# Scan phases moved among the outer products, x rows and raw weights asked for by ScalarE, bias products moved to the end of the first half

## The chip, the cores and the metric

The kernel runs on one core of one Trainium2 chip. The metric is the device time of one execution in microseconds; a figure for a kernel is the median of its runs. The profiled execution has a time of its own, given beside its span (first to last instruction). PE is TensorE (PEld its weight loads), DVE VectorE, ACT ScalarE, POOL GpSimd, SP SyncE, which here only starts transfers (SPq).

## The reference, cut to what matters

One layer of a hybrid decoder on 2048 tokens of width 1024. Only its first part is touched by the change: the RMSNorm of x, the combined projection, the tables that the state-space mixer is scanned with, and the vectors of the relative bias.

```python
h = rms_norm(x, norm1_g)                     # per token: x * rsqrt(mean(x*x) + eps) * g
P = h @ w_in                                 # 1024 x 1676, columns of groups A, u and C
A_bar = jnp.exp(A * dt)                      # 32 groups x 64 complex states
B_bar = ((A_bar - 1.0) / A)[..., None] * Bm
_, states = lax.associative_scan(_scan_combine, (a_seq, Bu), axis=1)
bias = bias_tbl[rel_bucket(dist)]            # for every distance, 8 heads
```

After it come the local and compressed attention, the output projection and a feed-forward part of width 4096, which the change leaves as they are, but for how one pool of tiles is declared.

## The kernel before, in words

All large products are made in three passes of a high and a low word (`mm3`, L81 to 85). `phase_front` (L94 to 303) makes the projection in two halves of 1024 tokens. Each half first makes the 512 columns of u, transposed (`u_step`, twice 96 matmuls of 512 columns), and then three chunks of columns, a, b and c (384, 384 and 396 wide), each for 8 tiles of 128 tokens: one `product` (L178) is 24 matmuls into one of two banks of PSUM (`ps_m`). ACT takes a bank out, scaled by the token's RMS factor `rx` (L190), and squares a part (L192), DVE sums the squares (L193), and POOL stores the row (L194). A product can start when the bank of the one before the last is out.

The factors `rx` come from `row_sum` (L115): a row of x of 512 KB is loaded and ACT sums its squares (L120). Rows 0 to 7 are loaded by SP during the second u step. Rows 8 to 15 are asked for by POOL, one after each product of chunk a: POOL copies one column of the evicted tile into the row's tile (L118) so that the load (L119) comes behind the eviction. `row_factors` (L122) makes 8 factors on DVE.

The raw weights of a chunk go through 3 buffers (`fetch_w`, L141, on SP) and are split by ACT (L154) and DVE (L155) in `keep_w`; for a, b and c of the first half these two are given a higher priority (`W_HOIST`, 300), so that the scheduler puts them early.

`ssm_tables` (L357) is a generator whose parts are merged between the steps of u and of chunk a. On DVE it makes powers 0 to 16 of the decay by one exponential over 17 x 32 values per partition (L399 and `exp_acc`), the sines (ACT, L349), the powers of the rotation, then the scan phases `Ea` and `Eb` by doubling (L431 to 446), and the matrices Y and W. `pair_steps` (L508) then makes, 16 times, an outer product on DVE (L519 to 521), a product on PE (`pk`, L528) and their stores; its steps are merged between the rest of a, b and c. The phases are first read in `table_steps` (L561), in the second half.

`bias_vectors` (L785) runs between the two parts of chunk a in program order: SP loads the table (`tab`) and six pieces of a one-hot matrix (`boh`), PE multiplies them (`bpr`, L797), ACT copies the result out and POOL stores it. Its tiles lie in a pool `bv` of their own, on memory that the tables' temporary tiles used before. `bias_rows` (L803) later spreads the result over 128 rows of DRAM (`rsw`, `r2w`, 5.1 MB written). At the start of the second half `rx` is turned by PE and written out (L227 to 231), and read back as `rxb` for the evictions of u.

Within `phase_front` the program order is a hint: a scheduler orders each engine's instructions at build time by its own estimate of when they can start, and the order is then fixed. Each engine and each queue works strictly in order.

Of the kernel before, what the change touches and what calls it, by code (L numbers as in the profile page):

```python
# [16 lines left out]
P = 128  # L17
# [76 lines left out]
def phase_front(tc, C, x, norm1_g, w_in, uT, pd, rh_a, prm, ssm_d, rx_d, consts, extra, later, x_t, r_last, last_bank):  # L94

    nc = tc.nc
    with ExitStack() as ctx:
# [15 lines left out]
        def row_sum(t, after=None):  # L113
            xr = rp.tile([P, D], F32, tag="x", name=f"x{t}", bufs=3)
            if after is None:  # L115
                nc.sync.dma_start(xr, xv[t])
            else:
                nc.gpsimd.tensor_copy(xr[:, 0:1], after)  # L118
                nc.gpsimd.dma_start(xr, xv[t])  # L119
            nc.scalar.activation(xr, xr, AF.Square, accum_out=ss[:, t:t + 1])  # L120

        def row_factors(half):  # L122
            sl = slice(8 * half, 8 * half + 8)
            with tc.high_priority(offset=W_HOIST):
                rsqrt_into(nc, rp, rx[:, sl], ss[:, sl], 1.0 / D, 8, "rq")

# [22 lines left out]
        def keep_w(half, kind, c0, n, k, raw):  # L149
# [3 lines left out]
            with tc.high_priority(offset=W_HOIST) if kind in "abc" and not half else nullcontext():  # L153
# [22 lines left out]
        open_, box_x, w_more = {}, [], []  # L176

        def product(t, hs, w, kind, c0, n, part=None):  # L178
# [29 lines left out]
        for half in range(2):  # L208
# [17 lines left out]
            if half:  # L226
                ptr = ps_t.tile([P, 512], F32, tag="pt", name="ptr")[0:NT, 0:P]  # L227
                nc.tensor.transpose(ptr, rx, C["ident"])
                rxt = sm.tile([NT, P], F32, tag="rxt", name="rxt", bufs=1)
                nc.scalar.copy(rxt, ptr)  # L230
                nc.gpsimd.dma_start(rx_d.rearrange("n r c -> (n r) c"), rxt)
                tables = table_steps(tc, C, S, ctx.enter_context(tc.tile_pool(name="sgt", bufs=1, side="right", reuse_waits="tile")), ps_t)
            c_x = ctx.enter_context(ExitStack())
            with tc.tile_pool(name=f"a_psu{half}", bufs=1, space=PSUM, reuse_waits="tile") as ps_u:
# [30 lines left out]
                if half == 0:  # L265
# [3 lines left out]
                    sums = [lambda t=t: row_sum(t) for t in range(8)] + [lambda: row_factors(0)]  # L269
# [9 lines left out]
            if half == 0:  # L279
                with tc.tile_pool(name="sg_ps0", bufs=1, space=PSUM, reuse_waits="tile") as ps_g:  # L280
# [76 lines left out]
def ssm_tables(tc, C, S, pool, first, prm, dkp):  # L357
# [17 lines left out]
    S.update(Y=Y, Yp=Yp, W=W, C1=C1, C2=C2, AR=AR, AI=AI, Ea=Ea, Eb=Eb, rho16=rho16, dD=dD)  # L375
# [4 lines left out]
    with ExitStack() as ctx2:  # L380
        tp2 = ctx2.enter_context(tc.tile_pool(name="si2", bufs=1))
        with ExitStack() as ctx:
# [11 lines left out]
            jt = C["ramp"]  # L394
            xr = tmp([P, 17, G], "xr")
# [3 lines left out]
            nc.vector.tensor_tensor(xr, adr.unsqueeze(1).broadcast_to([P, 17, G]), jt.unsqueeze(2).broadcast_to([P, 17, G]), op=ALU.mult)  # L399
            yield  # L400
            rho = exp_acc(nc, tp, xr, [P, 17, G], "e2")
            yield
            nc.vector.tensor_copy(rho16, rho[:, 16])
# [4 lines left out]
            sincos(nc, k, sc, th)  # L408

# [19 lines left out]

            yield  # L430
            nc.vector.tensor_scalar(sn[64:P, 4:11], sn[64:P, 4:11], -1.0, None, op0=ALU.mult)  # L431
            for E, j0, m in ((Eb, 4, 4), (Ea.rearrange("p g j a -> p j g a")[:, 1:3], 8, 3)):
                nc.vector.memset(E[:, 0, :, 0:1], 1.0)
                nc.vector.memset(E[:, 1, :, 0:1], 0.0)
                for j in range(m):
                    n = 2 ** j
# [2545 lines left out]
```

## Time and profile before

| | |
|---|---|
| median of 3 runs | 2428.22 us (2425.92 to 2432.09) |
| profiled execution | 2422.61 us, span 2420.8 us |
| PE busy | 2360.3 us, 97% of the span |
| DVE, ACT, POOL busy | 74%, 53%, 45% |
| mean granted clock of TensorE | 0.992 |

The whole kernel is bound by PE, so time is gained only where PE waits or runs at its lower clock. The granted clock is given as a share of 2.4 GHz: 1.00 is the upper level and 0.50 the lower one (1.2 GHz). The first half of the projection lies between 0 and 192 us of the span.

### The profile page before, as it was taken

Reading aid. Unit: us, or ns where it says so; the run is one execution under the profiler, and the core shown is the slowest. Engines: PE = TensorE matmul, PEld = TensorE weight load, DVE = VectorE, ACT = ScalarE, POOL = GpSimd, SP = SyncE. Lnnn points to the kernel's source line nnn. Section 1 sums busy time; section 2 is a strip of 40 time slices with the busy share of each in tenths; the row PEclk is TensorE's granted clock in tenths of the full one; section 3 lists DMA queues with packets and bytes.
Section 4 is the critical chain, followed back from the end, with each engine's and each line's share of the span. In section 5 each row is a group of like instructions: output and inputs, shape, how many; then the busy total and the mean of one; then the engine's idle time right before and its main releaser. Section 6 shows DMA issues by size and latency. Waiting matters only on the chain. (4 is left out here: it accounts for less than half of the span.)

```text
span 2420.8 us, 37163 instructions
## 1 busy us (share of the span) xinstructions
PE 2360.3 (97%) x12292; PEld 2019.6 (83%) x12292; DVE 1782.6 (74%) x3470; ACT 1294.4 (53%) x2726; POOL 1087.2 (45%) x1210
## 2 busy tenths in 40 slices
PE   8899999999899999999999999999999999999999
PEld 7798999787788889888788888888877888888887
DVE  7866885885877888886855557545567888888886
ACT  5443545775777676665655555544454344433442
POOL 1331122323443454332676665566562554545547
PEclk9899999999999999999999999999999999999999
DMA  8674554641322343112666677655548444344435
GB/s 269 179 253 140 179 157 144 168 151 53 129 75 79 92 120 118 43 56 96 196 205 195 195 217 215 191 158 147 148 145 272 135 130 123 100 138 133 128 102 197
DMA packets 409766, 361.60 MB, mean 149 GB/s; under 512 B 45132, under 2 KB 360290, under 8 KB 407492
## 3 DMA queue, kind: packets, MB, share of 16 engines
q1 hardware_dynamic: 355460, 295.83, 40.5%
q10 hardware_dynamic: 43296, 34.09, 4.5%
q0 software_dynamic: 10816, 29.31, 3.6%
q8 instruction: 97, 1.59, 0.3%
q14 instruction: 97, 0.79, 0.1%
HBM read 236.31 MB, written 128.02 MB: 150 GB/s over the span
## 5 line engine op out<-in xcount | busy, mean ns | idle before, releaser
L2228 ACT CAST v<-vr 128x512 fp32r<-128x512 f32 x224 | 139.4, 624 | 295.7 <-DMA vr<-vd 139.7
L2229 DVE TENSOR_TENSOR v<-vr,v 128x512 fp32r<-128x512 f32 x224 | 237.9, 1071 | 80.2 <-ACT v L2228 79.2
L2392 DVE TENSOR_TENSOR ul<-fs,uh 128x512 fp32r<-128x512 f32 x124 | 112.2, 923 | 104.7 <-ACT uh L2391 104.5
L2694 PE MATMUL pdc<-dw,v 128*128 128x512 f32 x768 | 184.9, 389 | 2.6 <-DVE acc L2715 2.6
L2694 PE MATMUL pda<-dw,v 128*128 128x512 f32 x768 | 184.8, 389 | 0.7 <-ACT acc0u L2700 0.7
L2694 PE MATMUL pdb<-dw,v 128*128 128x512 f32 x768 | 184.8, 389 | 0.0
L2694 PEld LDWEIGHTS pdc<-dw,v 128*128 128x128 f32 x768 | 144.0, 188 | 33.3 <-DVE acc L2715 3.4
L2694 PEld LDWEIGHTS pda<-dw,v 128*128 128x128 f32 x768 | 144.1, 188 | 31.0 <-ACT acc0u L2700 1.1
L2694 PEld LDWEIGHTS pdb<-dw,v 128*128 128x128 f32 x768 | 144.1, 188 | 30.3 <-DVE acc L2715 0.4
L2391 ACT CAST uh<-fs 128x512 fp32r<-128x512 f32 x124 | 74.3, 620 | 160.0 <-POOL fs L2380 123.2
L2392 DVE TENSOR_TENSOR ul<-ur,uh 128x512 fp32r<-128x512 f32 x93 | 87.9, 948 | 68.5 <-ACT uh L2391 68.5
L2539 POOL TENSOR_TENSOR ev<-ex,e 128x512 f32<-128x512 f32 x32 | 43.1, 1347 | 206.7 <-ACT ex L2522 206.7
L1662 ACT CAST ths<-pps 128x512 fp32r<-128x512 f32 (+1 forms) x144 | 79.0, 564 | 72.2 <-PE pps L1646 63.2
L2522 ACT ACTIVATE e<-e 128x512 f32<-128x512 f32 x128 | 81.0, 633 | 53.4 <-DVE e L2491 51.4
L1667 DVE TENSOR_TENSOR tls<-pps,ths 128x512 fp32r<-128x512 f32 (+1 forms) x144 | 92.6, 657 | 23.0 <-ACT ths L1662 22.2
L1997 PE MATMUL pw<-wo_h,mh 128*128 128x512 f32 x256 | 106.6, 416 | 1.2 <-DVE mx L2019 0.9
L2470 PE MATMUL pub<-fh,uh 128*128 128x512 f32 x256 | 101.7, 397 | 4.9 <-DVE e L2491 4.9
L1997 PE MATMUL pw<-wo_h,ml 128*128 128x512 f32 x256 | 104.6, 409 | 0.0
L1997 PE MATMUL pw<-wo_l,mh 128*128 128x512 f32 x256 | 104.2, 407 | 0.0
L2470 PE MATMUL puc<-fl,uh 128*128 128x512 f32 x256 | 99.8, 390 | 1.6 <-DVE fl L2410 1.5
L2470 PE MATMUL pub<-fh,ul 128*128 128x512 f32 x256 | 100.6, 393 | 0.0
L2470 PE MATMUL puc<-fh,ul 128*128 128x512 f32 x256 | 99.8, 390 | 0.7 <-DVE ul L2392 0.7
(581 smaller groups left out, 7604.0 us busy)
## 6 DMA issues: line engine op xcount, KB each, us to landing
vr<-vd SPq DMA_DIRECT2D x224, 256.0 KB
ur<-in_w_up SPq DMA_DIRECT2D x124, 256.0 KB
vd<-ev SPq DMA_DIRECT2D x96, 256.0 KB
vd<-e ACTq DMA_DIRECT2D x64, 256.0 KB
dr<-in_w_down SPq DMA_DIRECT2D x32, 512.0 KB
mx<-in_x ACTq DMA_DIRECT2D x32, 256.0 KB
x<-mx ACTq DMA_DIRECT2D x32, 256.0 KB
vd<-e SPq DMA_DIRECT2D x32, 256.0 KB
```

Of the source, the lines that this page charges most:

```text
L1662: yield "ACT", cast_ns(n), lambda: nc.scalar.copy(th[:, 0:nb], pt[:, 0:nb])
L1667: t = yield "DVE", sub_ns(n), lambda: nc.vector.tensor_tensor(tl[:, 0:nb], pt[:, 0:nb], th[:, 0:nb], op=ALU.subtract)
L1997: t = yield "PE", mm_ns(512), lambda: nc.tensor.matmul(pw[n], a[half][:, j], b[k][:, sl], start=k == 0 and m == 0, stop=k == NK - 1 and m ...
L2228: nc.scalar.copy(dh, src)
L2229: nc.vector.tensor_tensor(dl, src, dh, op=ALU.subtract)
L2391: yield "ACT", 621, lambda: self.nc.scalar.copy(h, src.tile)
L2392: t = yield "DVE", 900, lambda: self.nc.vector.tensor_tensor(l, src.tile, h, op=ALU.subtract)
L2470: nc.tensor.matmul(banks[b], w[:, j], h[:, j], start=k < 4 and j == 0 and i == 0, stop=j == HALF - 1 and i == 2, skip_group_check=True)
L2522: t = yield "ACT", 640, lambda: nc.scalar.activation(r, r, func)
L2539: t = yield "POOL", 1400, lambda: nc.gpsimd.tensor_tensor(E["v" + q].tile, E[x].tile, E[y].tile, op=op)
L2694: nc.tensor.matmul(bank[b, q], x[:, q, j], y[:, j], start=first and j == 0 and n == 0, stop=j == 1 and n == 2, skip_group_check=True)
```

## The change

The scan phases leave `ssm_tables` and become nine steps (`phase_steps`) that are merged over the later part of the outer products. The 17 powers of the decay come from one exponential of 32 values and four doublings. Rows 8 to 15 of x are asked for by ACT after the products of chunk b, and each is summed one product later. The first three raw weights of chunk b are loaded behind the first eviction of chunk a, and the split of b's weights loses its priority. The one-hot matrix is loaded by ACT in three pieces of up to 1024 columns into row tiles, and the bias products, five now, come among the last three products of chunk c. The turning of `rx` moves ahead of them. In `phase_down` five tiles of split weights are declared as one pool of five buffers instead of five pools' places.

```diff
-        def row_sum(t, after=None):
-            xr = rp.tile([P, D], F32, tag="x", name=f"x{t}", bufs=3)
+        def row_tile(name):
+            return rp.tile([P, D], F32, tag="x", name=name, bufs=3)
+        def row_load(t, after=None):
+            xr = x_row[t] = row_tile(f"x{t}")
             if after is None:
                 nc.sync.dma_start(xr, xv[t])
             else:
-                nc.gpsimd.tensor_copy(xr[:, 0:1], after)
-                nc.gpsimd.dma_start(xr, xv[t])
+                nc.scalar.copy(xr[:, 0:1], after)
+                nc.scalar.dma_start(xr, xv[t])
+        def row_sum(t):
+            xr = x_row.pop(t)
             nc.scalar.activation(xr, xr, AF.Square, accum_out=ss[:, t:t + 1])
...
+        def turned_factors():
+            ptr = ps_t.tile([P, 512], F32, tag="pt", name="ptr")[0:NT, 0:P]
+            nc.tensor.transpose(ptr, rx, C["ident"])
...
             raw = pool.tile([P, n], F32, tag="wraw", name=f"wr{half}_{kind}{c0}_{k}", bufs=bufs)
+            if (kind, half) == ("b", 0) and k < 3:
+                nc.scalar.copy(raw[:, 0:1], newest[0])
...
-            with tc.high_priority(offset=W_HOIST) if kind in "abc" and not half else nullcontext():
+            with tc.high_priority(offset=W_HOIST) if kind in "ac" and not half else nullcontext():
...
+            newest.append(o[:, 0:1])
             store(1)
-            if (kind, t // 8) == ("a", 0):
-                row_sum(t + 8, o[:, n:n + 1])
+            if (kind, t // 8) == ("b", 0):
+                row_load(t + 8, o[:, 0:1])
+                if t:
+                    row_sum(t + 7)
...
+                    bvp = []
+                    fetch, products = extra(kf, bvp, ps_t)
...
-                    with tc.tile_pool(name="bv", bufs=1, reuse_waits="tile") as bv:
-                        extra(bv, ps_t)
                     pre = c_pre.enter_context(tc.tile_pool(name="pre", bufs=1, side="right", reuse_waits="tile"))
+                    bvp.append(pre)
                     pairs = pair_steps(tc, C, S, ssm_d, pre, ps_g)
-                    run(merge(l2[n2:] + [lambda: row_factors(1)] + lists[1] + lists[2], pairs))
+                    l3 = lists[2][:2] + [lambda: (row_sum(NT - 1), row_factors(1))] + lists[2][2:3] + [lambda f=f: f(row_tile) for f in fetch] + lists[2][3:5] + [turned_factors] + merge(lists[2][5:], products)
+                    run(merge(merge(l2[n2:] + lists[1] + l3), merge([lambda: None] * 10 + phase_steps(tc, S, pre)), pairs))
...
-            nc.vector.tensor_tensor(xr, adr.unsqueeze(1).broadcast_to([P, 17, G]), jt.unsqueeze(2).broadcast_to([P, 17, G]), op=ALU.mult)
-            rho = exp_acc(nc, tp, xr, [P, 17, G], "e2")
...
+            e = exp_acc(nc, tp, adr, [P, G], "e2")
+            nc.vector.memset(rho[:, 0], 1.0)
+            nc.vector.tensor_copy(rho[:, 1], e)
+            for n in (1, 2, 4, 8):
+                nc.vector.tensor_tensor(rho[:, n + 1:2 * n + 1], rho[:, 1:n + 1], rho[:, n:n + 1].broadcast_to([P, n, G]), op=ALU.mult)
...
+def phase_steps(tc, S, tp):
+    def double(E, j0, j):
+        t = tp.tile([P, GB, 17, 16], F32, tag="ot", name=f"et{j0}{j}", bufs=1)...
+        nc.vector.tensor_tensor(e1, E[:, 0, :, 0:n], er, op=ALU.mult)
+        (five more, as L441 to L445 before)
+    return [start] + [lambda E=E, j0=j0, j=j: double(E, j0, j) for E, j0, m in parts for j in range(m)] + [end]
...
-    res = [lambda: None] * 5
+    res = [lambda: None] * 1
...
-def bias_vectors(tc, tp, ps, rel_bias, oh2, ohs, r2, rs):
+def bias_vectors(tc, first, tp, ps, rel_bias, oh2, ohs, r2, rs):
+    tab = first.tile([33, 8], F32, name="b_tab", bufs=1)
+    def fetch(j, row):
+        o = M[j] = row(f"boh{j}")
+        m = min(D, n2 - j)
+        nc.scalar.dma_start(o[0:33, 0:m], oh2[:, j:j + m])
+        if m < D:
+            nc.scalar.dma_start(o[0:33, m:m + n1], ohs)
+    def part(c0):
+        nc.tensor.matmul(pr[0:8, 0:n], tab, M[c0 // D * D][0:33, c0 % D:c0 % D + n], start=True, stop=True)
...
+    return [lambda row, j=j: fetch(j, row) for j in range(0, n2, D)], [lambda j=j: part(j) for j in range(0, n2, 512)]
...
-        w_high = pool("d_w2", 1)
-        w_last = pool("d_w3", 1)
+        w_high = pool("d_w2", 5)
```

## Rows read from the trace of the kernel before

**Rows 1.** The page: its busy shares, and the granted clock by 40 slices of 60.5 us.

```profile
PE 2360.3 (97%) x12292; PEld 2019.6 (83%) x12292; DVE 1782.6 (74%) x3470; ACT 1294.4 (53%) x2726; POOL 1087.2 (45%) x1210
...
PEclk9899999999999999999999999999999999999999
```

**Rows 2.** What PE waited for between 50 and 130 us: us in total, times, longest.

```profile
PE bpr L797 <- DMA boh<-in_k_oh: 6.6, 2, 5.3
PE pm_a L83 <- ACT po_a L190: 3.3, 1, 3.3
```

**Rows 3.** Busy time of the engines in the three gaps of PE, each followed by the stretch behind it: length, busy time (instructions) of PE, PEld, DVE, ACT and POOL, granted clock, share of the DMA engines, GB/s.

```profile
61.90:65.36 3.46, 0.14 (x2) 0.00 (x1) 1.87 (x9) 3.43 (x6) 0.00 (x0) 0.83 0.61 147
65.36:71.10 5.74, 5.74 (x18) 5.74 (x19) 5.60 (x21) 2.98 (x6) 2.18 (x6) 0.51 0.57 151
93.30:98.69 5.39, 0.06 (x1) 0.03 (x1) 5.20 (x11) 3.14 (x7) 0.90 (x2) 0.97 0.60 156
98.69:105.30 6.61, 6.61 (x18) 4.79 (x19) 6.18 (x11) 3.74 (x9) 3.79 (x5) 0.51 0.69 200
112.70:114.05 1.35, 0.08 (x2) 0.03 (x1) 0.78 (x3) 1.35 (x4) 0.00 (x0) 1.00 0.58 149
114.05:120.40 6.35, 6.35 (x20) 4.17 (x20) 4.77 (x20) 1.88 (x5) 2.69 (x6) 0.73 0.47 179
```

**Rows 4.** The same columns for chunk a, from its first matmul to the second gap.

```profile
53.48:93.30 39.82, 36.51 (x193) 35.93 (x191) 35.10 (x130) 18.18 (x33) 9.18 (x20) 0.91 0.57 163
```

**Rows 5.** PE in order of time (start, duration): the first matmul of products a0 and a1, the first behind the first gap with what ended it, and two successive groups of pair products, each behind a product of chunk b.

```profile
53.48 0.33 PE L83 MATMUL pm_a<-wh_a,hh 128*128 128x384 f32 x1
57.69 0.35 PE L83 MATMUL pm_a<-wh_a,hh 128*128 128x384 f32 x1
65.36 0.69 PE L83 MATMUL pm_a<-wh_a,hh 128*128 128x384 f32 x1 [3.31 <-ACT po_a L190]
147.57 1.02 PE L528 MATMUL pk<-oCA,k_Y 128*128 128x256 f32 x4
152.60 1.02 PE L528 MATMUL pk<-oCA,k_Y 128*128 128x256 f32 x4
```

**Rows 6.** ACT in order of time around the first gap.

```profile
61.62 0.61 ACT L154 ACTIVATE wh_b<-wr_b,g 128x384 fp32r<-128x384 f32 x1 [5.84 <-DMA wr_b<-in_w_in]
62.25 1.28 ACT L349 ACT_TABLE_LOAD   x1
64.75 0.56 ACT L190 ACTIVATE po_a<-pm_a,rx 128x384 f32<-128x384 f32 x1
```

**Rows 7.** Transfers started by SP, and DVE in order of time, around the second gap; the third row is one of SP's waits between 50 and 130 us.

```profile
96.06 0.34 SPq L790 DMA_DIRECT2D tab<-in_rel_bias  x1
96.45 0.42 SPq L795 DMA_DIRECT2D boh<-in_k_oh  x1
...
SPq L790 <- DVE t_v L490: 25.1, 1, 25.1
...
95.35 0.68 DVE L490 TENSOR_TENSOR t_v<-t_B,k_qi 128x512 f32<-128x512 f32 x1
98.44 0.07 DVE L789 MEMSET tab<- 1x8 f32 x1
```

**Rows 8.** The matmuls of the bias products, from the view of their tile: duration in ns least, median, most; first and last start.

```profile
L797 PE MATMUL bpr<-boh,tab x12: 482/522/921, 98.7 to 123.1; 33*8 33x432 f32 x10, 33*8 33x384 f32 x2
```

**Rows 9.** DVE: the exponential's two longest groups with 544 values, the same with 32 values, and the first and the last instruction of the scan phases (43 in all).

```profile
L321 DVE TENSOR_TENSOR e2t<-e2p,e2r x6: 725/726/726, 39.0 to 47.0; 128x544 f32<-128x544 f32 x6
L322 DVE TENSOR_SCALAR e2p<-e2t x6: 435/444/444, 41.6 to 49.9; 128x544 f32<-128x544 f32 x6
L321 DVE TENSOR_TENSOR e1t<-e1p,e1r x6: 129/191/193, 27.4 to 30.3; 128x32 f32<-128x32 f32 x6
...
77.63 0.20 DVE L440 TENSOR_TENSOR t_tp<-k_Eb,k_sc 128x32 f32<-128x32 f32 x1
92.49 0.28 DVE L446 TENSOR_SCALAR k_Ea<-k_Ea 128x256 f32<-128x256 f32 x1
```

**Rows 10.** The x rows: ACT's wait for them between 50 and 130 us, and the time from issue to landing (least, median, most) of the rows that POOL asks for; then the same of the stores `dca` of the outer products, which run from 106.6 to 171.9 us.

```profile
ACT x L120 <- DMA x<-in_x: 23.0, 7, 5.1
...
DMA to landing us min/median/max: 4.2/4.7/6.0
...
DMA to landing us min/median/max: 2.3/4.7/11.8
```

**Rows 11.** DVE in order of time: the first and the last instruction that make the factors of rows 8 to 15; the first waits for ACT's sum of row 15.

```profile
113.27 0.17 DVE L51 TENSOR_SCALAR rqh<-ss 128x8 f32<-128x8 f32 x1 [1.99 <-ACT x L120]
120.72 0.15 DVE L61 TENSOR_TENSOR rx<-rx,rqt 128x8 f32<-128x8 f32 x1
```

**Rows 12.** The first of the bias rows' four large transfers on SP (the other three follow from 137.37 us), the stretch of 25 us in which they run (columns as in Rows 3), ACT's longest wait for the weights of the second half behind them, the last split of the second half's x on DVE, and the first matmul of that half on PE.

```profile
126.00 0.52 SPq L806 DMA_DIRECT2D r2w<-r  x1
...
125.00:150.00 25.00, 25.00 (x140) 24.27 (x139) 15.26 (x30) 9.60 (x20) 9.65 (x18) 1.00 0.88 283
...
158.96 0.72 ACT L154 ACTIVATE wh_u<-wr_u,g 128x512 fp32r<-128x512 f32 x1 [5.13 <-DMA wr_u<-in_w_in]
182.88 1.23 DVE L129 TENSOR_TENSOR hl<-xT,hh 128x1024 fp32r<-128x1024 f32 x1 [1.54 <-ACT hh L128]
192.48 0.48 PE L83 MATMUL pu<-hh,wh_u 128*128 128x512 f32 x1
```

More of the change, by code (lines that the diff above doesn't have):

```diff
@@ L125, in row_factors @@
                 rsqrt_into(nc, rp, rx[:, sl], ss[:, sl], 1.0 / D, 8, "rq")
+        def turned_factors():
+            ptr = ps_t.tile([P, 512], F32, tag="pt", name="ptr")[0:NT, 0:P]
+            nc.tensor.transpose(ptr, rx, C["ident"])
+            rxt = sm.tile([NT, P], F32, tag="rxt", name="rxt", bufs=1)
+            nc.scalar.copy(rxt, ptr)
+            nc.gpsimd.dma_start(rx_d.rearrange("n r c -> (n r) c"), rxt)
         def half_words(h, l, raw):
@@ L226, in phase_front @@
             if half:
[L227 to L231, printed above, removed]
                 tables = table_steps(tc, C, S, ctx.enter_context(tc.tile_pool(name="sgt", bufs=1, side="right", reuse_waits="tile")), ps_t)
@@ L268, in phase_front @@
                     rp = c_rp.enter_context(tc.tile_pool(name="a_r", bufs=2, side="right", reuse_waits="tile"))
-                    sums = [lambda t=t: row_sum(t) for t in range(8)] + [lambda: row_factors(0)]
+                    sums = [lambda t=t: (row_load(t), row_sum(t)) for t in range(8)] + [lambda: row_factors(0)]
                     kf = c_rp.enter_context(tc.tile_pool(name="a_kf", bufs=1, side="right", reuse_waits="tile"))
@@ L498, in ssm_tables, with start, end @@
         nc.vector.tensor_tensor(dD, dT.unsqueeze(2).broadcast_to([16, G, 16]), C["ident"][0:16, 0:16].unsqueeze(1).broadcast_to([16, G, 16]), op=ALU.mult)
+def phase_steps(tc, S, tp):
+    nc = tc.nc
+    Ea, Eb, sn, cs = S["Ea"], S["Eb"], S["sc"][:, 0], S["sc"][:, 1]
+    parts = (Eb, 4, 4), (Ea.rearrange("p g j a -> p j g a")[:, 1:3], 8, 3)
+    def start():
+        nc.vector.tensor_scalar(sn[64:P, 4:11], sn[64:P, 4:11], -1.0, None, op0=ALU.mult)
+        for E, _, _ in parts:
+            nc.vector.memset(E[:, 0, :, 0:1], 1.0)
+            nc.vector.memset(E[:, 1, :, 0:1], 0.0)
+    def double(E, j0, j):
+        n = 2 ** j
+        t = tp.tile([P, GB, 17, 16], F32, tag="ot", name=f"et{j0}{j}", bufs=1).rearrange("p i t q -> p (i t q)")[:, 0:16 * G].rearrange("p (i n g) -> p i n g", i=2, g=G)
+        er = cs[:, j0 + j].unsqueeze(2).broadcast_to([P, G, n])
+        ei = sn[:, j0 + j].unsqueeze(2).broadcast_to([P, G, n])
+        e1, e2 = (t[:, i, 0:n].rearrange("p n g -> p g n") for i in range(2))
+        nc.vector.tensor_tensor(e1, E[:, 0, :, 0:n], er, op=ALU.mult)
+        nc.vector.tensor_tensor(e2, E[:, 1, :, 0:n], ei, op=ALU.mult)
+        nc.vector.tensor_tensor(E[:, 0, :, n:2 * n], e1, e2, op=ALU.subtract)
+        nc.vector.tensor_tensor(e1, E[:, 0, :, 0:n], ei, op=ALU.mult)
+        nc.vector.tensor_tensor(e2, E[:, 1, :, 0:n], er, op=ALU.mult)
+        nc.vector.tensor_tensor(E[:, 1, :, n:2 * n], e1, e2, op=ALU.add)
+    def end():
+        nc.vector.tensor_scalar(Ea[:, :, 0], Ea[:, :, 2], -1.0, None, op0=ALU.mult)
+    return [start] + [lambda E=E, j0=j0, j=j: double(E, j0, j) for E, j0, m in parts for j in range(m)] + [end]
 GB = 2
@@ L2762, in trunk @@
           cmp_pos, cmp_w1, cmp_w2, out_norm_g, w_out, norm2_g, w_up, w_down,
-          k_ident, k_ramp, k_oh2, k_ohs, k_blk, k_forced, k_wmask, k_rows31, k_sel, x_t, out, dbg=None):
+          k_ident, k_oh2, k_ohs, k_blk, k_forced, k_wmask, k_rows31, k_sel, x_t, out, dbg=None):
     nc = tc.nc
@@ L2775, in consts @@
             nc.sync.dma_start(C["ident"], k_ident)
-            for n, src in (("ramp", k_ramp), ("forced", k_forced), ("rows31", k_rows31)):
+            for n, src in (("forced", k_forced), ("rows31", k_rows31)):
                 C[n] = cp.tile(list(src.shape), F32, name="c_" + n)
@@ L2784, in consts, with biases @@
                 nc.vector.tensor_scalar(gains[:, j:j + 1], gains[:, j:j + 1], 0.125, None, op0=ALU.mult)
-        def biases(tp, ps):
-            bias_vectors(tc, tp, ps, rel_bias, k_oh2, k_ohs, r2, rs)
+        def biases(first, tp, ps):
+            return bias_vectors(tc, first, tp, ps, rel_bias, k_oh2, k_ohs, r2, rs)
         pd = {kind: dr.tile([L, n], F32, name="p" + kind) for kind, n in WIDTHS.items()}
```

58 lines of the change are left out of this document (18 added, 40 removed).

## The prediction

> **What bounds the kernel now.** I read the page first, then the waits of PE, then its stages. The page says that PE is busy for 97% of the span and that no other engine comes near [rows 1]: time is gained only where PE stands still or runs at its lower clock. In the clock line of the page a single digit, that of the second slice of 60.5 us, is below 9 [rows 1], so I asked for PE's waits between 50 and 130 us. There are three gaps there [rows 2]: one of 3.3 us for an eviction of chunk a, and two, 6.6 us in all, for the one-hot matrix of the bias products. The windows around them show the second half of the price [rows 3]: behind each gap the granted clock falls to the lower level, 1.2 GHz, though PE is busy without a break (5.74 us at 0.51, 6.61 us at 0.51, 6.35 us at 0.73). Chunk a agrees. One product takes 57.69 - 53.48 = 4.21 us at the upper level [rows 5], eight take 33.7 us, and the chunk took 39.82 us up to the second gap [rows 4]; the 6.1 us between are the first gap and the slow stretch behind it.
>
> Why the gaps are there is read from the other engines' order. First gap: product a2 needs the bank of a0, and ACT, which works in order, stood 5.84 us for raw weights of chunk b (put early by their priority), then loaded its table for the sine, and evicted a0 only at 64.75 us, 7 us after a0 was done at about 57.7 [rows 5, 6]. Second gap: the bias tiles lie on memory of the scan tables, so SP waited 25.1 us for DVE's last use of it (the instruction at 95.35), asked for table and matrix at 96, and DVE wrote the table's last row at 98.44 [rows 7]; PE, in order, had the bias product ahead of chunk b. Third gap: the fourth piece of the matrix came 1.3 us late [rows 2, 3].
>
> **The change part by part.**
>
> *First gap.* Without the priority, the split of b's weights no longer stands ahead of a0's eviction, and their first three loads come behind it by the copy on ACT. The sine moves ahead of the exponential, so ACT meets it some 15 us before a0 is done, where ACT waits for x rows anyway. The gap's 3.31 us go [rows 2], and with it the slow stretch: 5.74 x (1 - 0.51) = 2.8 us [rows 3]. What is late next? The weights of b are needed when chunk b starts, 33.7 us behind the start of a; the gate opens about 5 us into that time and eight loads through three buffers follow. In the trace a load that SP starts is split within a few us, so I cost this at nothing. If ACT waits for such a load ahead of the next eviction, it has one product, 4.2 us, before PE feels it.
>
> *Second and third gap.* The bias products go to the end of chunk c, their table is loaded early into memory of its own, and their matrix is asked for at least two products of c (over 8 us) ahead. The gaps' 6.6 us go [rows 2], and the slow stretches: 6.61 x 0.49 = 3.2 us and 6.35 x 0.27 = 1.7 us [rows 3]. The products themselves cost the same: 5 x 432 + 384 = 2544 columns before, 4 x 512 + 496 = 2544 after; 12 matmuls of 0.52 us are 6 us at most [rows 8], and the new ones the same by their columns. What comes later is `r2w` and `rsw`, below.
>
> *Exponential.* With 544 values a pair of its steps takes 0.73 + 0.44 us, with 32 values about 0.19 + 0.18 [rows 9]; over the 23 instructions and the product with the ramp that is about 13.8 us against 4.2, plus 1.3 for four doublings and copies: 8 us of DVE saved. DVE is not what PE waits for at that time, so I cost this at nothing; it only makes the tables earlier.
>
> *Scan phases.* 43 instructions, 77.6 to 92.8 us, with little between them [rows 9]: some 14 us of DVE leave chunk a and return among the outer products. There PE waits for no DVE result. DVE is busy for 15.26 of 25 us in the stretch of 125 to 150 us [rows 12], and the outer products start earlier by what left; no cost. If that cover were gone, the 14 us would delay the pair products, which nothing reads before the second half. The phases themselves are first read in the second half too.
>
> *x rows 8 to 15.* They move from POOL after a's products to ACT after b's. ACT loses 23.0 us of waiting [rows 10] that hid under chunk a. It gains eight issues, eight copies of one column (about 0.2 us each) and the same eight squares. A period of chunk b with its pair product is 152.60 - 147.57 = 5.0 us [rows 5]. By my estimate from these durations a row is asked for about 1.7 us after a product (eviction 0.56 [rows 6], square, copy, issue) and summed at about 2.2 us after the next, 5.5 us later; it lands in 4.7 us (4.2 to 6.0) [rows 10], so ACT waits for half a microsecond at most, against 4.2 us that it may be late. Cost nothing; bounds are nothing, and the case below in which the rows land late. The Trainium skill (DMA: Bandwidth & Descriptors, "Issuing engines are not separate DMA queues") speaks against a gain here: transfers started by any engine run on the same 16 DMA engines, and another issuer saves only the time to issue. By that rule 4.2 MB more share chunk b's stretch with the stores of the outer products, which land after 4.7 us and up to 11.8 us [rows 10]; no run shown has them together, and it is why I give the late landing below some chance.
>
> *Turned factors.* They wait for `row_factors(1)`, whose DVE chain took 113.27 to 120.87, 7.6 us [rows 11]. In the new order three products of c, 13 us, lie between the last row's sum and the transpose. That leaves some 4 us for the last row's landing and its sum; no cost.
>
> *Bias rows to DRAM.* 5.1 MB written in 126 to 145 us move behind the later bias products, some 25 to 40 us. They are 4 writes of 1.08 MB and 4 of 0.19 MB. Before, the DMA engines were at 0.88 in their stretch, and behind them ACT waited 5.13 us for a weight of the second half without PE feeling it [rows 12]. After, they meet the loads of the second half's x. The last of these was split at 184.1 us, and PE started that half at 192.48 [rows 12]: 8.4 us of slack against some 15 us of transfer that is shared. Bounds: nothing, or up to 7 us. I take 2 us, nearer to nothing, because SP's loads of x come first in program order.
>
> *Pool in `phase_down`.* Five tiles per chunk rotate over five buffers in the same order as before, each again in the same place: nothing.
>
> *Sum.* Gaps 3.3 + 6.6 = 9.9; clock 2.8 + 3.2 + 1.7 = 7.7; together 17.6 us less, 2 us given back: 15.6. The waits of PE after 250 us are for other engines' results, which move with it, so I let the whole shift reach the end. On the profiled execution that is 2422.6 - 15.6 = 2407.0 us; its time lies 5.6 us below the median of the runs shown, so the forecast for a median is 2428.2 - 15.6 = 2412.6, say 2412.
>
> **The rivals.**
>
> *B: the bias rows collide with the second half's loads.* For it: the 8.4 us of slack are less than the transfer, and the x loads go through few buffers. Against it: the first row of those waits was hidden before, and the scheduler may put the transfers later still. Price 7 us and a slow stretch of 2.8 us behind it: 2428.2 - 17.6 + 9.8 = 2420.4.
>
> *C: the first gap stays.* ACT could stand for b's weights (now loaded later) ahead of an eviction of chunk a, or for the sine. For it: ACT is in order, and 5.84 us is what it stood before [rows 6]. Against it: the split is now behind two evictions in program order. Then 6.1 us are not gained: 2428.2 - 15.6 + 6.1 = 2418.7.
>
> *D: the new places wait for transfers, and it gets slower.* The bias products, and the transpose ahead of them, stand in PE's order in chunk c behind three loads of the matrix on ACT's queue. These stand behind the sum of x row 15, and so behind that row's landing. It decides at a landing of about 8.5 us (two products of c): above that PE stands at each of the three pieces. If each costs what the second gap did, 5.34 + 3.2 us, that is 25.6 us: 2428.2 - 17.6 + 25.6 = 2436.2. For it: stores in that stretch landed in up to 11.8 us [rows 10], and rows of x are added. Against it: the 5.1 MB of bias rows leave just that stretch, and the median there is 4.7 us.
>
> **How the numbers follow.** Forecast (both kinds of gap go, little returns) 0.60; B 0.19; C 0.09; D 0.12. About 0.3%, 7.3 us here, is what a measurement can tell from no change. The forecast and C lie beyond it, B is on its edge (half and half), D is beyond it on the other side but for a sixth: faster 0.60 + 0.08 + 0.09 = 0.77, which I lower to 0.75 for what the scheduler does elsewhere with the same code; same 0.15; slower 0.10. The range starts at the full 17.6 us and the 2.3 us by which runs shown lie below their median, with some 3 us for cover that I did not see: 2405. It ends at 2429, which holds B, C and no gain at all, and leaves out most of D.
>
> **What would show it.** In the profile after: no wait of PE above 1 us between 50 and 180 us, and the granted clock at 1.00 there; a0 evicted within 1 us of its end near 58 us; chunk b's first matmul at 87 to 88 us instead of about 100; the second half's first matmul near 175 to 177 us instead of 192.48; the scan phases on DVE between outer products after 95 us; ACT waiting under 1 us for each of x rows 8 to 15. B would show as a wait of `pu` for `hh` or `wh_u` behind `r2w`; C as a wait of `pm_a` for `po_a`; D as waits of `bpr` or `ptr` in chunk c. The forecast is wrong if the second half starts at 177 us and the span is still longer than 2412: then the shift was lost later.

## The result, and the profile after

The changed kernel takes 2413.43 us (median of 4 runs, 2411.59 to 2414.61), against 2427.07 us for the kernel before beside it: a ratio of 0.9941 (95% interval 0.9923 to 0.9959). A second comparison, made later, gave 0.9959 (0.9947 to 0.9971). The forecast was 2412, and by its total it was right. The traces show that this was luck: only about half of the gain comes from where it was expected, and the other half from a term that the prediction put at nothing.

Two lines of the changed kernel's page, which answer to [rows 1].

```profile
PE 2358.1 (98%) x12290; PEld 2019.3 (84%) x12290; DVE 1775.4 (74%) x3475; ACT 1295.4 (54%) x2736; POOL 1075.4 (45%) x1194
...
PEclk9999999999899999999999999999999999999999
```

Then what PE waited for between 50 and 215 us (us in total, times, longest), as in [rows 2].

```profile
PE pk L559 <- ACT kst L563: 2.7, 1, 2.7
PE pm_a L83 <- ACT po_a L207: 2.2, 1, 2.2
PE pu L83 <- DVE uo L188: 1.6, 1, 1.6
PE pk L559 <- DVE oCA L552: 1.6, 1, 1.6
```

The waits for `boh` are gone and the second slice of the clock is full. But four waits stand where there were two kinds; the page's slices of 60 us don't show them. The windows behind the first of them in time and around the next two (columns as in [rows 3]):

```profile
77.30:82.00 4.70, 4.70 (x18) 4.70 (x19) 2.33 (x5) 2.44 (x5) 0.54 (x1) 0.64 0.86 259
...
145.00:150.00 5.00, 2.32 (x12) 1.84 (x11) 3.01 (x16) 2.96 (x6) 0.18 (x1) 1.00 0.16 47
150.00:155.00 5.00, 5.00 (x20) 4.78 (x19) 4.93 (x16) 2.30 (x6) 1.43 (x3) 0.66 0.51 161
...
160.00:165.00 5.00, 3.73 (x17) 2.39 (x16) 5.00 (x10) 2.63 (x6) 1.09 (x2) 1.00 0.51 147
```

Each of the first two gaps (2.2 us up to 77.3 us, 2.7 us up to 149.6 us) has a slow stretch behind it, as the old ones had: 0.64 and 0.66 where PE is busy without a break, which is another 1.7 us each. What ended them is read from ACT in order of time (the last row belongs to the second half):

```profile
73.55 0.62 ACT L171 ACTIVATE wh_b<-wr_b,g 128x384 fp32r<-128x384 f32 x1 [1.53 <-DMA wr_b<-in_w_in]
75.49 1.24 ACT L171 ACTIVATE wh_b<-wr_b,g 128x384 fp32r<-128x384 f32 x2 [1.32 <-DMA wr_b<-in_w_in]
76.64 0.56 ACT L207 ACTIVATE po_a<-pm_a,rx 128x384 f32<-128x384 f32 x1
...
138.58 0.33 ACTq L124 DMA_DIRECT2D x<-in_x  x1
...
145.47 1.06 ACT L128 ACTIVATE x<-x 128x1024 f32<-128x1024 f32 x1 [4.48 <-DMA x<-in_x]
...
207.19 0.62 ACT L171 ACTIVATE wh_a<-wr_a,g 128x384 fp32r<-128x384 f32 x1 [10.41 <-DMA wr_a<-in_w_in]
```

and from DVE in the same way:

```profile
69.16 0.61 DVE L172 SCALAR_TENSOR_TENSOR wl_b<-wr_b,g,wh_b 128x384 fp32r<-128x384 f32 x1
...
146.65 0.17 DVE L51 TENSOR_SCALAR rqh<-ss 128x8 f32<-128x8 f32 x1 [5.34 <-ACT x L128]
...
148.76 0.17 DVE L562 TENSOR_TENSOR kst<-pk,k_dD 16x32 f32<-16x32 f32 x1
...
208.37 2.48 DVE L188 TENSOR_TENSOR uo<-pu,rxb 128x512 f32<-128x512 f32 x4
```

ACT's wait for x rows 8 to 15 (85 to 150 us):

```profile
ACT x L128 <- DMA x<-in_x: 22.2, 8, 4.5
```

At 77 us ACT has three splits of b's weights ahead of an eviction; their raw weights come late, because the three buffers are freed by splits on DVE, the first at 69.16. At 147 us ACT has stood 4.48 us for x row 15, asked for at 138.58, and DVE 5.34 us for its sum; the add of a pair product (`kst`, L562) stands behind that on DVE, ACT's copy of the product behind the add, and PE behind the copy. Near 209 us ACT has stood 10.41 us for a raw weight of chunk a, DVE for its split, and the evictions `uo` behind that. SP in order of time shows that this weight travels beside the large bias rows: it is asked for 2.3 us behind the first of them, and ACT can start on it 8.6 us later (198.63 to 207.19).

```profile
196.35 0.60 SPq L848 DMA_DIRECT2D r2w<-r  x1
198.63 0.34 SPq L162 DMA_DIRECT2D wr_a<-in_w_in  x1
```

Marks of PE tell where a shift arises and where it is lost. The table has starts in us: of the first and last product of u in the second half, of the last product of c, and of the last products of the up and down projections (`pub`, `pdc`), for all kernels that ran. The first half of the changed kernel varies from one execution to the next: with the same code up to there, `first u` was 185.5, 182.9, 181.2 and 183.0 (the changed kernel twice, e2 and e6). Differences of 2 us between single profiles are therefore not read as effects in that column.

| kernel | first u | last u | last c | last pub | last pdc | ratio to before |
|---|---|---|---|---|---|---|
| before | 192.5 | 236.8 | 400.6 | 1801.3 | 2413.0 | 1 |
| changed | 185.5 | 231.8 | 397.6 | 1789.0 | 2403.4 | 0.9941 (0.9923 to 0.9959) |
| changed, again | 182.9 | 228.6 | 394.7 | 1786.9 | 2402.0 | 0.9959 (0.9947 to 0.9971) |
| e1 before, one pool | 192.6 | 236.9 | 401.4 | 1793.7 | 2408.2 | 0.9975 (0.9966 to 0.9984) |
| e2 changed, old pools | 181.2 | 227.4 | 393.6 | 1793.9 | 2407.1 | 0.9973 (0.9961 to 0.9985) |
| e3 x rows earlier | 180.1 | 226.2 | 392.1 | 1784.2 | 2400.2 | 0.9949 (0.9935 to 0.9963) |
| e4 b's weights by POOL | 182.8 | 229.2 | 396.5 | 1790.2 | 2404.8 | 0.9972 (0.9960 to 0.9984) |
| e5 gate | 180.9 | 227.2 | 393.2 | 1786.5 | 2402.2 | 0.9949 (0.9936 to 0.9961) |
| e6 r2w at 291 us | 183.0 | 227.4 | 396.6 | 1790.5 | 2405.2 | 0.9958 (0.9944 to 0.9971) |
| e7 phases early | 178.6 | 225.0 | 391.2 | 1782.1 | 2396.5 | 0.9940 (0.9925 to 0.9954) |
| e8 three edits | 180.3 | 224.7 | 396.5 | 1791.1 | 2405.5 | 0.9956 (0.9942 to 0.9970) |
| e9 e7, r2w from 342 us on | 182.3 | 226.8 | 392.2 | 1787.8 | 2402.1 | 0.9942 (0.9929 to 0.9955) |
| e10 gate, phases over b, r2w late | 175.5 | 219.9 | 385.4 | 1780.5 | 2394.8 | 0.9918 (0.9905 to 0.9931) |

The changed kernel starts its second half 7.0 us earlier (9.6 in the second profile), not 15 to 17; by the end of chunk c only 3.0 us of it are left (6.0). Then, at about 1797 us, 6.7 us are won at one stroke, in a place that the prediction costed at nothing (the last output projection `pw` is 5.6 us earlier than before, the last `pub` 12.3). Between the end of chunk c and `pw` 2.6 us come back that no run explains; e1, whose code is that of the kernel before up to there, has 1.5 us of them too.

### The profile page after: what moved, and what is told of

It reads as the page before. It is cut to its first block, busy times and chain, and to the rows that moved or that the text cites. A ratio compares the mean times of both kernels' runs of the same rounds, so it can differ in the third digit from the quotient of the medians.

```text
span 2412.8 us, 37142 instructions
## 1 busy us (share of the span) xinstructions
PE 2358.1 (98%) x12290; PEld 2019.3 (84%) x12290; DVE 1775.4 (74%) x3475; ACT 1295.4 (54%) x2736; POOL 1075.4 (45%) x1194
## 5 line engine op out<-in xcount | busy, mean ns | idle before, releaser
L2039 PE MATMUL pw<-wo_l,mh 128*128 128x512 f32 x256 | 104.0, 406 | 0.0
L2512 PE MATMUL puc<-fh,uh 128*128 128x512 f32 x256 | 100.1, 391 | 0.0
```

Of the source, the lines that this page charges most:

```text
L2039: t = yield "PE", mm_ns(512), lambda: nc.tensor.matmul(pw[n], a[half][:, j], b[k][:, sl], start=k == 0 and m == 0, stop=k == NK - 1 and m ...
L2512: nc.tensor.matmul(banks[b], w[:, j], h[:, j], start=k < 4 and j == 0 and i == 0, stop=j == HALF - 1 and i == 2, skip_group_check=True)
```

## The experiments

**e1 and e2: the pool of `phase_down`.** e1 is the kernel before with this edit alone, e2 the changed kernel without it.

```diff
-        w_high = pool("d_w2", 1)
-        w_last = pool("d_w3", 1)
+        w_high = pool("d_w2", 5)
...
-                t = home[o][0].tile([P, 2, 2, N], F32R, tag=home[o][1], name=f"dw{c}{o}")
+                t = (w_low if o in ORDER[:2] else w_high).tile([P, 2, 2, N], F32R, tag="w", name=f"dw{c}{o}")
```

> The kernel before with one edit: in phase_down the five tiles of split weights are declared as one pool of five buffers. Theory (the declaration lets the scheduler place the splits dw behind the eviction e, and that is where some of the late gain is from): the wait of pub for DVE e of 4.72 us near 1797 us is gone, the last pub starts about 6 us earlier than at 1801.3 us, and the time is about 4 us shorter, a ratio of 0.998. Rival (the declaration is worth nothing, as the prediction costed it; the late gain is the shift from the front): the wait stays, the marks stay within 1 us of those of the kernel before, ratio 1.000.

> The changed kernel with the pools of phase_down as they were before, all else as changed. Theory (declaration is worth 4 us or more, the front some 3 us where chunk c of the second half ends): the wait of pub for DVE e comes back near 1791 us, last pub near 1796 us, time about 2424 us less 4, ratio 0.9985 against the kernel before and 4 to 6 us longer than the changed kernel. Rival (front gives it all): no such wait, ratio 0.994 as for the changed kernel.

The theory held for both, though e2 came out shorter than its 0.9985. DVE in order of time in the kernel before:

```profile
1787.70 4.40 DVE L2229 TENSOR_TENSOR dw<-dt,dw 128x1024 fp32r<-128x1024 f32 x2
1792.02 3.37 DVE L2229 TENSOR_TENSOR dw<-dr,dw 128x1024 fp32r<-128x1024 f32 x1
...
1796.56 0.68 DVE L2491 TENSOR_TENSOR e<-pub,e 128x512 f32<-128x512 f32 x1
```

the longest wait of its PE between 1770 and 1830 us:

```profile
PE pub L2470 <- DVE e L2491: 4.7, 1, 4.7
```

and the windows of that wait and of what is behind it (columns as in [rows 3]):

```profile
1792.00:1797.30 5.30, 0.57 (x4) 0.15 (x2) 5.22 (x4) 1.07 (x2) 2.31 (x1) 0.76 0.15 48
1797.30:1803.00 5.70, 5.70 (x16) 4.57 (x17) 1.96 (x4) 3.81 (x7) 0.00 (x0) 0.62 0.32 96
```

DVE in order of time in e1:

```profile
1787.09 0.69 DVE L2491 TENSOR_TENSOR e<-pub,e 128x512 f32<-128x512 f32 x1
...
1803.71 4.75 DVE L2229 TENSOR_TENSOR dw<-dt,dw 128x1024 fp32r<-128x1024 f32 x2
```

and what PE waits for in e1 between 1770 and 1830 us:

```profile
PE pdc L2690 <- ACT dw L2228: 2.8, 1, 2.8
PE pdc L2690 <- DVE dw L2229: 1.2, 1, 1.2
```

Before, some 9 us of splits stand ahead of the eviction `e` on DVE, PE waits 4.7 us for it, and the clock falls to 0.62 behind. With one pool `e` comes at 1787.09 and the splits behind it. The last `pub` is 7.6 us earlier, the last `pdc` 4.8, since it is now `pdc` that waits for splits. In e2 the 4.7 us are back. The edit is worth 0.25%, 6.1 us (3.9 to 8.2); all the others together 0.27%, 6.5 us (3.6 to 9.5). The sum, 12.6 us, is what the changed kernel gains (14 us in the first comparison, 10 in the second).

**e3: x rows asked for four products earlier.**

```diff
-            if (kind, t // 8) == ("b", 0):
-                row_load(t + 8, o[:, 0:1])
-                if t:
-                    row_sum(t + 7)
+            i = {("a", 0): t - 4, ("b", 0): t + 4}.get((kind, t // 8), -1)
+            if 0 <= i < 8:
+                row_load(i + 8, o[:, 0:1])
+            if 0 < i <= 8:
+                row_sum(i + 7)
+            if i == 8:
+                row_factors(1)
```

> The changed kernel with x rows 8 to 15 asked for four products earlier (behind products 4 to 7 of chunk a and 0 to 3 of chunk b), each summed one product later, and the factors made behind product 4 of chunk b. Theory (the gap of 2.68 us before pk at 149.6 us and the slow stretch behind it come from ACT's wait for x row 15 and from the chain of the factors on DVE that stands for that sum): no wait of PE above 1 us between 140 and 160 us, granted clock 1.00 in 145 to 155, the second half starts 3 to 4.5 us earlier than at 185.5 us. Rival 1 (DVE is simply full there with scan phases and splits of weights): the gap stays at about its place with 2 to 3 us. Rival 2 (the rows meet the raw weights of chunk b): the gap at 77 us grows, and the second half starts no earlier.

Between 130 and 180 us PE did not wait and the clock was 1.00, and the second half started 5.4 us earlier than in the first profile of the changed kernel. But ACT now stood for a raw weight of c ahead of the eviction of chunk a at 96.17 us (that the rows held this weight up is not shown):

```profile
95.64 0.62 ACT L171 ACTIVATE wh_c<-wr_c,g 128x396 fp32r<-128x396 f32 x1 [3.77 <-DMA wr_c<-in_w_in]
```

and PE felt it in chunk b (two of its waits between 50 and 215 us):

```profile
PE pm_b L83 <- ACT po_a L207: 1.8, 1, 1.8
PE pm_b L83 <- ACT po_b L207: 1.2, 1, 1.2
```

The time stayed that of the changed kernel. The gap at 147 us is tied to row 15 by all nine profiles of the late rows together. In each of them ACT stood 3.3 to 5.1 us for that row. Where its sum began 13.9 and 14.0 us behind the start of chunk c (changed, e9), PE waited 2.7 and 2.6 us; where it began after 9.0 to 11.6 us (the other seven) PE waited 1.0 us at most. Why the row is summed so much later in some executions stays open.

**e4 and e5: the gap at 77 us.** e4 changes who asks for b's raw weights; e5 puts all of them behind evictions.

```diff
-            return [... fetch_w(half, kind, c0, n, k, sp, 3, nc.sync)) for k in ks]
+            return [... fetch_w(half, kind, c0, n, k, sp, 3, nc.gpsimd if (kind, half) == ("b", 0) else nc.sync)) for k in ks]
```

```diff
             if (kind, half) == ("b", 0) and k < 3:
                 nc.scalar.copy(raw[:, 0:1], newest[0])
+            elif (kind, half) == ("b", 0):
+                nc.gpsimd.tensor_copy(raw[:, 0:1], newest[-1])
```

> The changed kernel with the raw weights of chunk b of the first half asked for by POOL instead of SP. Theory (the gap of 2.15 us at 77 us and the slow stretch behind it come from SP, which stands with the loads of the second half's x, waiting for DVE, ahead of the raw weights of b that ACT's order has ahead of an eviction of chunk a): no wait of pm_a for po_a above 0.5 us between 65 and 90 us, clock 1.00 there, chunk b starts near 89 us instead of 92.3 us. Rival (the gate behind the first eviction is itself too late, whoever asks): the gap stays within 1 us of its size.

> The changed kernel in which the raw weights 3 to 7 of chunk b of the first half are also asked for behind an eviction (POOL copies one column of the newest evicted tile of chunk a into their buffer), so that the scheduler can put at most two of their splits ahead of the next eviction. Theory (the gap at 71 to 77 us comes from the order on ACT: splits of b's weights 3 to 5 stand ahead of the eviction of product 3, and their buffers are freed by splits on DVE, which is full with the tables until about 69 us): the wait of pm_a for po_a falls below 0.7 us, the granted clock is 1.00 from 65 to 90 us, chunk b starts at 88.5 to 89.5 us instead of 92.3 us. Rival (a split of any of these weights that stands ahead of an eviction costs the same, wherever it stands): a gap of 2 to 4 us stays, one product later, near 81 us.

e4's theory fell, and its rival is not shown either, since the gap grew by 1.6 us. POOL and then ACT in order of time in e4, and SP in the changed kernel:

```profile
64.61 0.55 POOL L211 DMA_DIRECT2D pa<-po_a  x1 [5.29 <-DVE po_a L210]
65.21 1.06 POOL L162 DMA_DIRECT2D wr_b<-in_w_in  x2
...
71.34 1.26 ACT L171 ACTIVATE wh_b<-wr_b,g 128x384 fp32r<-128x384 f32 x2 [6.40 <-DMA wr_b<-in_w_in]
...
69.80 7.79 SPq L162 DMA_DIRECT2D wr_b<-in_w_in  x10
```

What PE waits for between 60 and 95 us in e4:

```profile
PE pm_a L83 <- ACT po_a L207: 3.8, 1, 3.8
```

and in e5:

```profile
PE pm_a L83 <- ACT po_a L209: 1.2, 1, 1.2
```

In e4 ACT stood 6.40 us for the third weight of b. POOL asked for it only at 65.21 us, because the store of a row stood ahead of it in POOL's order, and that store waited 5.29 us for DVE. So e4 put another wait in the place of the one that it was to remove, and it does not test SP's queue. The changed kernel's own trace settles that: SP asks for the weight that ends up late at 69.80 us, right behind the end of DVE's first split (69.16 + 0.61), and ACT can start on it at 73.55. The queue is not the cause there; the order on ACT and the late split on DVE are. The Trainium skill (DMA: Bandwidth & Descriptors, "Issuing engines are not separate DMA queues") says that another issuer saves only the time to issue. In e4 nothing was gained by it: from POOL's asking to ACT's start it took 6.1 us (65.21 to 71.34), against 3.8 with SP. In e5 the clock stayed at 1.00 from 65 to 90 us, but 1.2 us is above the forecast and not enough to show that the gate helps: with the changed kernel's own first half the wait was 2.2, 2.1, 2.3 and, in e6, 1.4. Early phases without the gate had 2.7 and 3.2 us (e7, e9), and e10 with it has 0.5; that speaks for the gate, from one profile each.

**e6: the bias rows r2w later.** They go by POOL's queue, each behind one word of an evicted tile.

```diff
+                for f in later[:4]:
+                    f()
+                wide = [lambda: None] * 4 + [lambda f=f: f(newest[-1]) for f in later[4:]] + [lambda: None] * 4
...
-        lambda h=h: nc.sync.dma_start(r2w[h], r2[4 + h:5 + h].to_broadcast([P, 2160])) for h in range(4)]
+        lambda o, h=h: (nc.gpsimd.dma_start(r2w[h, 0:1, 0:1], o[0:1]), nc.gpsimd.dma_start(r2w[h], r2[4 + h:5 + h].to_broadcast([P, 2160]))) for h in range(4)]
```

> The changed kernel in which the four large bias rows r2w are written by POOL's queue, each behind a single word of an evicted tile of the second half, so that they come at about 290 to 350 us instead of 196 to 210 us; the output is the same. Theory (4 us of the gain are given back in the second half, and part of it because r2w stands on SP ahead of the last raw weight of a and fills the DMA engines, so that ACT waits 10.4 us for that weight, DVE for its split, and the evictions uo come late): the wait of pu for uo of 1.6 us is gone, ACT's wait for wr_a near 200 us falls from 10.4 to below 5 us, the DMA share of 200 to 220 us falls from 0.84 to near 0.5, and from the first pu of the second half to the last pm_c it is 1.5 to 3 us less than 212.1 us. Rival (the second half is slower for its order on DVE and ACT, whatever the transfers do): the wait for uo goes but waits of py and pv grow by as much, and the stretch stays within 1 us of 212 us.

Half of the theory held. The stretch of 200 to 220 us (columns as in [rows 3]) in the changed kernel:

```profile
200.00:220.00 20.00, 18.36 (x83) 14.89 (x82) 8.95 (x15) 3.06 (x5) 3.05 (x4) 1.00 0.84 284
```

and in e6:

```profile
200.00:220.00 20.00, 20.00 (x94) 16.55 (x93) 10.82 (x17) 4.26 (x7) 3.05 (x4) 1.00 0.39 102
```

The wait for `uo` went, and the u steps of the second half took 44.4 us instead of 46.3. But the longest waits of DVE and of PE in e6 between 290 and 320 us are new:

```profile
DVE hnhn L51 <- DMA hnhn<-pa: 3.1, 1, 3.1
...
PE py L688 <- DVE St L679: 3.2, 1, 3.2
```

The transfers, from 291.2 us on, had another victim: the small read `hnhn`, asked for at 292.69 us, held DVE, and DVE held PE. From `first u` to `last c` it took 213.7 us, more than the changed kernel's 212.1.

**e7: phases early.**

```diff
-merge([lambda: None] * 10 + phase_steps(tc, S, pre))
+merge(phase_steps(tc, S, pre) + [lambda: None] * 10)
```

> The changed kernel with the scan phases merged from the first outer product on (ten empty steps behind them instead of ahead of them), so that they end near 125 us instead of 165 us. Theory (the gap of 1.6 to 2.5 us before pk near 155 to 165 us is DVE full with the later phases, the splits of the second half's weights and words, so the phases are not free there): the wait of pk for DVE oCA is below 0.5 us, DVE is busy for less than 12 of 15 us in 150 to 165 us, the second half starts 1.5 to 2.5 us earlier. Rival (the gap is the late chain of the factors on DVE alone, and phases weigh nothing): the gap stays at 1.5 us or more, DVE as full as before.

The window of 150 to 165 us in e7:

```profile
150.00:165.00 15.00, 15.00 (x74) 12.41 (x73) 12.23 (x22) 8.32 (x16) 5.67 (x12) 1.00 0.74 239
```

and in the second profile of the changed kernel:

```profile
150.00:165.00 15.00, 12.12 (x52) 10.02 (x51) 14.93 (x35) 7.70 (x15) 5.90 (x11) 0.89 0.63 186
```

With the phases gone DVE is busy for 12.23 (forecast: under 12) instead of 14.93 of 15 us, PE does not wait, and the clock does not fall; the second half starts 4.3 us before that of the second profile. In e3, which keeps the phases there but has the factors earlier, the wait is gone too, though DVE is busy for 14.69 us in this window. So a full DVE is not enough. In the second profile it had also stood 6.0 us for the sum of row 15 (5.34 in the first), and was full, 9.93 of 10 us, from 145 us on; in e3 it was busy for 7.58 us of these 10. It took both, the time lost to the row and the phases; without either one PE does not wait. The time was 2409.4 us, and the intervals do not part it from the changed kernel.

**e8: e3 (with sums two products behind), e5 and e6 together.**

> The changed kernel with three edits together: x rows 8 to 15 asked for four products earlier and each summed two products later; the gate of all raw weights of b; the late r2w. Theory (gaps of the first half and the collision in the second are separate and add up): no wait of PE above 1 us between 50 and 200 us, second half starts at 176 to 178 us, time 7 to 9 us below the changed kernel's, ratio 0.990 to 0.991. Rival (a gap closed is opened elsewhere: in-order ACT or DVE then waits for another transfer): second half starts at 180 us or later, ratio 0.993 or more.

The rival held. Two of PE's waits between 50 and 420 us:

```profile
PE py L693 <- DVE St L684: 2.9, 1, 2.9
...
PE pm_b L83 <- ACT po_a L209: 2.1, 1, 2.1
```

The new waits that e3 and e6 had alone came along, and the second half lost some 4 us (216.1 us from `first u` to `last c`), about what the first had won (5.2 and 2.6 us against the two profiles of the changed kernel).

**e9, e10 and the changed kernel again.** In e9 the phases are early and r2w is written from 342 to 369 us, at the end of chunk b of the second half and in chunk c; e10 has r2w there too, all gates of e5, and the phases over chunk b (four empty steps ahead of them, six behind).

> The changed kernel with the phases merged from the first outer product on, and the four r2w rows on POOL's queue behind evictions of chunk c of the second half (about 330 to 365 us), away from the raw weights of the second half and from the small read hnhn near 292 us. Theory (r2w costs the u steps of the second half 2 us where it stands in the changed kernel, and cost chunk b 3 us when it was moved beside hnhn; in chunk c nothing reads beside it): from the first pu to the last pu of the second half 44.3 us instead of 46.3, from the last pm_a to the last pm_b 63 to 64.6 us, last pm_c near 389 us, time 1.5 to 2.5 us below the kernel with early phases alone. Rival (the transfers find another victim wherever they stand): a wait of PE of over 1 us in 330 to 400 us that no kernel before had, last pm_c at 391 us or later.

> The kernel of the run before in this call, with the phases merged over chunk b alone (four empty steps ahead of them, six behind), and the gate for all raw weights of chunk b. Theory (phases are free only where DVE has room, which is chunk b: DVE busy for some 22 of 40 us in 90 to 130 us; and the gate keeps the first gap at 1.2 us): no wait of PE above 1.3 us between 50 and 200 us, chunk b starts at 89.5 us, the second half at 176 to 177 us, last pm_c at 386 to 387 us, time 2418 less 12 for the median in the units of the kernel before at 2424, a ratio of 0.9925 to 0.9935. Rival (what is gained in the first half is given back in the second, as in the runs with rows earlier): last pm_c at 390 us or later, ratio 0.994 or more.

> The changed kernel as it is, beside the two others on the same chip. Theory (the gap of 2.68 us before pk at 149.6 us hangs on when x row 15 lands, which differs from one execution to the next, since a kernel with the same first half did not have it): the second half starts between 181 and 186 us, and its last pm_c comes 212 us after; ratio 0.993 to 0.995. Rival (the gap is fixed by the order, as in the first profile): the second half starts at 185 to 186 us again, with that wait.

What PE waited for from 50 to 255 us in the changed kernel again:

```profile
PE pv L659 <- DVE U L646: 2.5, 1, 2.5
PE pk L559 <- DVE oCA L552: 2.4, 1, 2.4
PE pm_a L83 <- ACT po_a L207: 2.1, 1, 2.1
...
PE pk L559 <- ACT kst L563: 1.0, 2, 0.6
```

and in e10:

```profile
PE pv L664 <- DVE U L651: 1.8, 1, 1.8
PE pm_a L83 <- ACT po_a L209: 0.5, 1, 0.5
```

The window of 50 to 200 us in the changed kernel again, and the stretch behind its wait for `oCA`:

```profile
50.00:200.00 150.00, 144.38 (x743) 132.27 (x742) 105.36 (x255) 71.80 (x142) 36.95 (x67) 0.99 0.64 194
161.10:166.00 4.90, 4.87 (x17) 4.54 (x18) 4.41 (x14) 2.21 (x4) 2.66 (x5) 0.65 0.84 228
```

and in e10:

```profile
50.00:200.00 150.00, 149.49 (x776) 137.07 (x775) 109.54 (x260) 72.01 (x143) 42.32 (x76) 1.00 0.64 197
```

e10 has what was forecast for the change itself: PE busy for 149.49 of 150 us at 1.00, and a second half that starts at 175.5 us. It took 2404.23 us (2401.66 to 2404.71), a ratio of 0.9918, and beats the kernel before and, in the same comparison, the changed kernel. What each of its three edits is worth was not run one by one. In e9 the u steps took 44.4 us and the stretch from `first u` to `last c` 209.9 us against 212.1, without a new wait above 1 us from 330 to 400 us. But `last c` came at 392.2 us, not near 389, and the time is not below that of e7: in the profiled execution row 15 came late (PE waited 2.6 us for `kst`) and the first gap was 3.2 us long; how often this happens in the other executions is not known. That r2w costs the u steps 2 us where the change puts it is clear from the table: 45.7 to 46.4 us in the seven profiles that have it there, 44.4 in the six that have not. In the changed kernel again the start of the second half and the wait for `kst` (1.0 us) were those of the theory; the ratio, 0.9959, was not (0.993 to 0.995), though its interval reaches there.

## Why the prediction was right, and where it was not

- *Second and third gap*: right. The bias products cost nothing where they are now, and none of the eleven profiles of the new order shows PE waiting for them or for `ptr` (50 to 250 us).
- *First gap*: the eviction of a0 came on time, at 58.34 us. But "it has one product, 4.2 us, before PE feels it" counted one late load; ACT's order has three splits ahead of one eviction, and DVE freed their buffers late. Of 6.1 us, 2.2 us of wait and 1.7 us of slow clock came back: rival C's mechanism, later and smaller.
- *x rows*: the failed figure is "ACT waits for half a microsecond at most". It waited 22.2 us for the eight rows. The landing was estimated well: a row could be summed 3.7 to 7.2 us after it was asked for, 4.8 us in the median, where the estimate had 4.7 [rows 10]. What failed is the 5.5 us between asking and summing: in the order that was built ACT stood at the sum 1.5 to 3.4 us after asking, and half of the rows were asked for only when the sum of the row before began. For row 15 it stood there after 2.4 us, and the row took 6.9 us (138.58 to 145.47). That is the late landing of rival D, but it struck the pair products by way of DVE's order, not `bpr` or `ptr`, and not in every execution.
- *Scan phases*: "there PE waits for no DVE result" was wrong. DVE had room in 125 to 150 us [rows 12], but the phases also fell into 150 to 165 us, beside the splits of the second half and behind the time that DVE had lost to row 15, and PE waited 1.6 and 2.5 us for `oCA`. Behind the longer wait the clock was 0.65, behind the shorter one 1.00.
- *Bias rows*: 2 us given back was right (the u steps took 46.3 us instead of 44.4), and so was the kind of cause. But what came late beside r2w was a raw weight of chunk a, not the loads of the second half's x.
- *Sum*: the new gaps of the first half cost 2.2 + 2.7 + 1.6 us of waits and twice 1.7 us of slow clock, 9.9 us; that leaves 7.7 of the 17.6 us, and the second half started 7.0 us earlier. "I let the whole shift reach the end" failed too. Besides r2w some 2 us more go in the second half: from `last u` to `last c` 165.8 and 166.1 us, against 163.8 before. Waits of `pv` and `py` are longer there (5.0 us against 4.0 in all), and one of 2.6 us has a slower clock behind it (0.74 from 303.5 to 310 us); why, no run settled. So the front gave 6.5 us, not 15.6.
- *Pool in `phase_down`*: "nothing" was wrong by 6.1 us. The tiles rotate as before, but the declaration moved the splits in DVE's order. By luck this term makes up for two thirds of the 9.1 us that are missing from the front; hence the right total.
- *Chances*: half of rival B's 0.19 is 0.095, not 0.08; the total hardly changes by it.

The sign that was written down (second half at 175 to 177 us, no wait above 1 us) was not met, and the total alone would have hidden it. That e10 meets it shows that the estimate of the gaps was sound, and that the cover was not: less the 6.1 us of the pool, its 21.1 us (16.7 to 23.0) leave 15 us for the front, where 15.6 was forecast.

## What to carry to other kernels

When a gap is closed, follow each instruction that moved to the engine where it now stands in order, and ask what is behind it if its transfer is 2 us later than usual; "off the critical path" has to be read from the stretch that it moves to, to its last microsecond. Read the slack of a transfer from the order in which its engine really asks and uses, not from the program: here the landing was estimated well and the slack was not. Bulk writes that nobody waits for need a place as much as loads do: look for a stretch in which no small read is due. And an edit that only declares memory can reorder an engine, so compare the order of each engine, not only the tiles.

## What was not expected of the hardware

In two kernels a small strided read was late beside a bulk write of another queue: `hnhn` (48 KB, on SP), asked for 1.5 us (e6) and 1.4 us (e8) behind a row of 1.1 MB on POOL's queue, held DVE for 3.1 and 2.9 us and was used 6.6 and 6.5 us after asking. In the eleven other profiles DVE used it 3.3 to 3.5 us after asking and did not wait. The same 512 KB of x that landed within 4.2 to 6.0 us in the kernel before [rows 10] took up to 7.2 us in the changed kernel (from 104.0 us on, the DMA engines busy for 0.71) and 7.5 us in its second profile (from 133.7 us on, 0.74).
